# One state chain of four groups in three slots a chunk, V placed beside U by identity products, and TensorE in the written order

## The chip, the cores and the metric

The kernel runs on one core of one Trainium2 chip, in one launch. The metric is the device time of that launch in microseconds (us), lower is better. Engines: PE is TensorE (its queue of weight loads is PEld), DVE is VectorE, ACT is ScalarE, POOL is GpSimd, SP issues most of the DMAs.

## What is computed

A two-layer hybrid backbone over 256 context tokens and 1024 latent tokens of width 1024. Layer 0 runs RWKV-7 time mixing (8 heads, both directions) and an order-2 Hyena long convolution (512 channels) side by side on one input projection; layer 1 is differential attention; each ends with a mixture of experts. The change lies in layer 0. The time mixing is a recurrence on a 64x64 state per head and direction:

```python
def step(s, inp):
    r_t, w_t, k_t, v_t, kk_t, a_t = inp
    sa = jnp.einsum('bhij,bhj->bhi', s, kk_t)
    s = (s * w_t[:, :, None, :]
         - sa[..., None] * (kk_t * a_t)[:, :, None, :]
         + v_t[..., None] * k_t[:, :, None, :])
    return s, jnp.einsum('bhij,bhj->bhi', s, r_t)
...
z = x1 * (fft_long_conv(v, kf[:, 0]) + v * hy_b[0])
return x2 * (fft_long_conv(z, kf[:, 1]) + z * hy_b[1])
```

The filters `kf` of the Hyena come from a small network, times a decay, divided by the sum of their absolute values, and transformed to frequencies.

## The kernel before

**The recurrence in chunks.** Tokens go in 40 chunks of 32 (C), two of them (WIN) a window, 20 windows (NW). The 8 heads are four groups of two; a head (h) and a direction (d) of a group is a quad, 32 partitions of a tile. Before the chain, each group is prepared (`rw_prep`): per chunk the arrays ar, G, bt, and T, the inverse of a triangular 32x32 matrix. `inverses` (L807) makes T on DVE by back substitution, 60 dependent ops on tiles N and Xt, and sends it to DRAM.

**The chain** (`rw_chain`, L870) loads a window's ar, G, T, bt, and V into one half of the tile uv, by SP. Then per chunk: pA, 16 products of G with V, copied by ACT to gv; then, for each of two chains of two groups (NS, GS): pr, the decayed state, on POOL; 8 products of ar with the state S into pc; rh on DVE; 8 products of T with rh; four copies of 32x128 of the result U into the other half of uv, two by DVE (L923) and two by ACT; 8 products of bt with uv, where U and V lie below one another in 64 partitions; and the new S on DVE, L141 (the shared line of all tensor_tensor ops). Last, pY: 32 products of G with uv and of ar with the old S add up to the chunk's output, which ACT copies to yw and SP stores. An fp32 product is two records in the trace.

**The fill** (`fill`, L2003) is what runs beside the chain: the rest of the input projection (`rest`, L685: the Hyena's columns i = 3 to 11, tile pj, which DVE mixes over neighbouring tokens into u, and the last inverses), the Hyena's filters (`filt`, L398, tile fps), the Hyena itself (`stage_hy`, tile hps), and steps of the adaLN projection (adaps). All large products are in three parts of an fp32r split, high x high, low x high and high x low (L171 to L173).

A filter's values are made in a loop over j (L426 to L441): two products of 512 columns, fbt on DVE, and on POOL two adds into nacc and two into EO; after 2 or 8 j the sum nacc is reduced by a product with ones (L443), by which all values are then scaled.

```python
self.tt(self.g, na, na, ab[:, 0], OP.add)
self.tt(self.g, na, na, ab[:, 1], OP.add)
self.tt(self.g, Eo[:, 0, j], fbt[:, 0], fbt[:, 1], OP.add)
self.made = self.tt(self.g, Eo[:, 1, j], fbt[:, 0], fbt[:, 1], OP.subtract).ins
yield 4
```

**What sets the order.** `weave` (L1998) steps through two lists of generators, the chain with the readout behind it (`rw_out`) and the fill, and always takes the one that has done the smaller share of its total: 64 (RWN) against 2509. What a generator yields is counted as done. This gives the order in which the program is written. The order on each engine is then set by a scheduler that simulates the program's times (`schedule_with_timeline_sim=True`, L2077), PE included.

Of the kernel before, what the change touches and what calls it, by code (L numbers as in the profile page):

```python
# [10 lines left out]
F32 = mybir.dt.float32  # L11
# [14 lines left out]
C = 32  # L26
NCH = NT // C
WIN = 2
# [94 lines left out]
class Net:  # L123
# [274 lines left out]
    def filt(self, p1, pw, pv, tabs, pp):  # L398
# [8 lines left out]
        for seg, (j0, nt) in enumerate(((0, 2), (2, 8))):  # L407
            for o in range(2):
                E = []
                for half in range(2):  # L410
# [71 lines left out]
    def filt_lat(self, pv, tabs, pw, pp, E, o):  # L482
# [3 lines left out]
        for cls in range(4):  # L486
            th, tl = next(tabs)
            for Eo, rn, cs in E:
                ko = pw.tile([128, 5, 256], F32, name="ko", bufs=1)
                for e in range(2):  # L490
# [9 lines left out]
                    yield 24 if cls else 12  # L500
# [16 lines left out]
class Net2(Net):  # L517
# [34 lines left out]
    def proj(self, w_src, ncol, hi, lo, wp, pp, toks, evac):  # L552
        raw = wp.tile([128, 8, 128], F32, name="wraw", bufs=1)
        self.sy.dma_start(raw[:, :, :ncol], w_src.rearrange("(k p) n -> p k n", p=128))
        wh = wp.tile([128, 8, 128], F32R, name="whi")
        wl = wp.tile([128, 8, 128], F32R, name="wlo")
        self.split(wh[:, :, :ncol], wl[:, :, :ncol], raw[:, :, :ncol])
        for t0, n in toks:
            ps = pp.tile([128, 512], F32, name="pj")
            self.mm3(ps[:ncol, :n], [((wh[:, k, :ncol], wl[:, k, :ncol]), (hi[:, k, t0:t0 + n], lo[:, k, t0:t0 + n])) for k in range(8)])  # L560
            evac(ps[:ncol, :n], t0, n)
# [38 lines left out]
    def stage_a2(self, pools, er, wp, hi, lo, pp):  # L600
# [23 lines left out]
        def run(c0, ncol, out, w0, w1, w2, b=None):  # L624
# [4 lines left out]
            self.proj(win[:, c0:c0 + ncol], ncol, hi, lo, wp, pp, TOK3,  # L629
# [26 lines left out]
        def hyena(i, bp, pt):  # L656
            u = up.tile([128, GG], F32, name="u")
            run(RWC + 128 * i, 128, u, self.c("cw", i), self.c("cw", 12 + i), self.c("cw", 24 + i), self.c("cb", i))
# [34 lines left out]
        return rest()  # L693

# [150 lines left out]
NS = 2  # L845
GS = 4 // NS
RPA = 1
# [3 lines left out]
class Net3(Net2):  # L851
# [3 lines left out]

    def rw_chains(self, es):
        a, v, g = self.a, self.v, self.g
        self.dram("y", [2, 2, GG, 4, 64])
        self.rp = self.pool(es, "rw", 2, side="right")
        self.rq = q = self.pool(es, "rwq", 2, side="right")  # L860
        self.rps = self.pool(es, "rwp", 1, PSUM, side="right")
        st = []
        for s in range(NS):
            x = q.tile([128, 2, GS, 64], F32, name=f"S{s}")
            v.memset(x, 0.0)
            st.append(x)
        for w in range(NW):
            st = yield from self.rw_chain(w, st)

    def rw_chain(self, w, st):  # L870

        v, g, pe, dr, p, q = self.v, self.g, self.pe, self.dr, self.rp, self.rq
# [4 lines left out]
        uv = p.tile([128, 2, WIN, 4, 64], F32, name="uv")  # L877
        yw = p.tile([128, WIN, 4, 64], F32, name="yw", bufs=1)
        for d in range(2):
# [3 lines left out]
            for h in range(2):  # L883
# [3 lines left out]
                self.sy.dma_start(uv[r0:r0 + 32, d].rearrange("s i g v -> s i (g v)"),  # L887
# [3 lines left out]
        quads = [(qd, qd // 2, qd % 2, slice(32 * qd, 32 * qd + 32), slice(64 * (qd // 2), 64 * (qd // 2) + 64)) for qd in range(4)]  # L891
        for i in range(WIN):
            ps = self.rps.tile([128, 4, 64], F32, name="pA", bufs=RPA)
            for gr in range(4):
                for qd, h, d, qs, hs in quads:
                    ms = slice(64 * h + 32 * (1 - d), 64 * h + 32 * (1 - d) + 32)
                    pe.matmul(ps[qs, gr], G[ms, d, gr, i, 0:C], uv[ms, d, i, gr], start=True, stop=True, tile_position=(ms.start, 32 * qd))
            gv = q.tile([128, 4, 64], F32, name="gv")
            self.act(gv, ps, AF.Copy)
            new = []  # L900
            for s in range(NS):
                gs = range(GS * s, GS * s + GS)
                S = st[s]
                pr = q.tile([128, 2, GS, 64], F32, name=f"pr{s}", bufs=1)
                for d in range(2):
                    db = self.dcoef[:, GS * s:GS * s + GS, d, CS[d][w] + i].unsqueeze(2).to_broadcast([128, GS, 64])
                    self.tt(g, pr[:, d], S[:, d], db, OP.mult)
                ps = self.rps.tile([128, GS, 64], F32, name=f"pc{s}")
                for j, gr in enumerate(gs):
                    for qd, h, d, qs, hs in quads:  # L910
                        pe.matmul(ps[qs, j], ar[hs, d, gr, i, 0:C], S[hs, d, j], start=True, stop=True, tile_position=(64 * h, 32 * qd))
                rh = q.tile([128, GS, 64], F32, name=f"rh{s}", bufs=1)
                self.stt(v, rh, ps, -1.0, gv[:, GS * s:GS * s + GS], OP.mult, OP.subtract)
                ps = self.rps.tile([128, GS, 64], F32, name=f"pc{s}")
                for j, gr in enumerate(gs):
                    for qd, h, d, qs, hs in quads:
                        pe.matmul(ps[qs, j], T[qs, i, gr], rh[qs, j], start=True, stop=True, tile_position=(32 * qd, 32 * qd))
                for qd, h, d, qs, hs in quads:
                    o = uv[qs, d, i, GS * s:GS * s + GS]
                    if qd % 2:  # L920
                        self.act(o, ps[qs], AF.Copy)
                    else:
                        v.tensor_copy(o, ps[qs])  # L923
                ps = self.rps.tile([128, 2, GS, 64], F32, name=f"pc{s}")
                for d in range(2):
                    for j, gr in enumerate(gs):
                        for h in range(2):
                            hs = slice(64 * h, 64 * h + 64)
                            pe.matmul(ps[hs, d, j], bt[hs, d, i, gr], uv[hs, d, i, gr], start=True, stop=True)
                x = q.tile([128, 2, GS, 64], F32, name=f"S{s}")  # L930
                self.tt(v, x, ps, pr, OP.add)
                new.append(x)
            ps = self.rps.tile([128, 4, 64], F32, name="pY")
            for gr in range(4):
                for qd, h, d, qs, hs in quads:
                    pe.matmul(ps[qs, gr], G[hs, d, gr, i, C:], uv[hs, d, i, gr], start=True, stop=False, tile_position=(64 * h, 32 * qd))
                    pe.matmul(ps[qs, gr], ar[hs, d, gr, i, C:], st[gr // GS][hs, d, gr % GS], start=False, stop=True, tile_position=(64 * h, 32 * qd))
            self.act(yw[:, i], ps, AF.Copy)
            st = new
            if i < WIN - 1:  # L940
                yield 1
        for qd, h, d, qs, hs in quads:
            c0 = CS[d][w]
            self.sy.dma_start(dr["y"][d, h, C * c0:C * (c0 + WIN)].rearrange("(i t) g v -> t i (g v)", t=C), yw[qs].rearrange("t i g v -> t i (g v)"))
        yield 1
        return st
# [66 lines left out]
class Net4(Net3):  # L1013
# [15 lines left out]
    def spec(self, p, pp, th, tl, hi, lo, tiles, yh, yl):  # L1029

        for ks, cr, ci, kr, ki, kr2, re, im in tiles:
# [3 lines left out]
            self.cmul(p, ps, kr, ki, kr2, yh, yl, re, im)  # L1035
            yield 6 * len(ks)
# [80 lines left out]
    def hy_lat(self, p, pw, tabs, pp):  # L1117
# [7 lines left out]
        for o in range(2):  # L1125
# [4 lines left out]
            for cls in (0, 2, 1, 3):  # L1130
# [18 lines left out]
                for acc, (yh, yl) in zip(accs, ys):  # L1149
                    av = acc.rearrange("p (m a) w -> p m a w", m=2) if o else acc.rearrange("p (a b) w -> p b a w", b=2)  # L1150
                    for m in range(2):
# [9 lines left out]
                        self.stage2(cls, av[:, m], ps[:, 0], ps[:, 1], pw, W)  # L1161
                        yield 24 if cls else 12
# [819 lines left out]
class Weave:  # L1982
    RWN = 64
# [19 lines left out]
def fill(net, es, rest):  # L2003
# [3 lines left out]
    with ExitStack() as es:  # L2007
        pp = net.pool(es, "fillp", 3, PSUM)
# [73 lines left out]
```

## Time and profile before

| | |
|---|---|
| median of 3 runs | 4129.59 us (4128.44 to 4133.65) |
| the profiled execution | 4128.25 us, span 4126.4 us |
| mean granted clock of PE | 0.934 |
| busy: DVE, ACT, POOL | 2876.1, 1881.8, 1033.5 us |
| DMA | 858.90 MB, mean 208 GB/s |

The profiled execution is one of the kernel's ordinary runs. The span counts from its first to its last instruction. Busy shares are averages over stages of different kinds; the stage of the change is cut out in the rows below. There a matmul's own duration is longer than the distance to the next one, since they are pipelined: costs on PE are read from start to start. A record with a number behind it (x32) stands for that many of one kind in a row.

### The profile page before, as it was taken

To read this page: it belongs to the slowest core of one execution; us is meant where nothing else is said; L and a number is where in the kernel's file an instruction comes from. 1 tells how busy PE (TensorE), PEld (TensorE's weight loads), DVE (VectorE), ACT (ScalarE), POOL (GpSimd) and SP (SyncE) were. 2 spreads that over 40 slices of the span, in tenths; PEclk is the share of its full clock that TensorE was granted. 3 is DMA by queue.
4 is the path that set the end of the run, shared out by engine and by line. 5 is a ranking of instruction groups with operands and counts; after the bars stand their busy time and mean duration, and the time that the engine had idled before them with its cause. 6 is when DMAs were issued, how large, how long until landed. Compare 5 with 4: busy or idle time off the path is not lost.

```text
span 4126.4 us, 75212 instructions
## 1 busy us (share of the span) xinstructions
PE 3731.2 (90%) x29980; PEld 2949.6 (71%) x29980; DVE 2876.1 (70%) x4269; ACT 1881.8 (46%) x3029; POOL 1033.5 (25%) x1186
## 2 busy tenths in 40 slices
PE   7988888789898999799999997989999787999996
PEld 4866666557677887577777776778887675777775
DVE  5378887556656775577777775157777646899997
ACT  4344443233322222165656664244444421777775
POOL 1165553263523441201111101212223111011100
PEclk9988998789798999799999998999999997999998
DMA  5234346666566677578878874254434545899996
GB/s 162 65 110 123 101 111 186 184 199 196 146 204 215 196 267 243 184 265 291 297 285 292 300 280 135 93 123 113 122 99 118 184 165 214 326 383 382 383 369 215
DMA packets 532010, 858.90 MB, mean 208 GB/s; under 512 B 161665, under 2 KB 337563, under 8 KB 527050
## 3 DMA queue, kind: packets, MB, share of 16 engines
q1 hardware_dynamic: 508704, 754.97, 54.4%
q0 software_dynamic: 19904, 90.55, 7.7%
q10 hardware_dynamic: 3050, 8.56, 0.5%
q8 instruction: 236, 3.87, 0.4%
q14 instruction: 116, 0.95, 0.1%
HBM read 708.00 MB, written 145.95 MB: 207 GB/s over the span
## 4 chain that ended last, share of the span: by engine, by line
PE 52%; issue 18%; DVE 13%; DMA 6%; POOL 5%; ACT 3%; SPq 1%; ACTq 0%; DVEq 0%; POOLq 0%
PE pj L171 4%; PE pj L173 4%; PE pj L172 4%; PE S L1828 3%; PE ps L1405 3%; PE ps L1406 3%; PE ps L1404 3%; DVE mx L1809 2%; PE ops L171 2%; PE ops L172 2%; PE ops L173 2%; PE py L1405 1%; PE py L1404 1%; PE py L1406 1%; PE tps L1824 1%
## 5 line engine op out<-in xcount | busy, mean ns | idle before, releaser
L141 DVE TENSOR_TENSOR wrl<-wr,wrh 128x1024 fp32r<-128x1024 f32 x762 | 924.2, 1223 | 202.1 <-ACT wrh L144 169.7
L144 ACT ACTIVATE wrh<-wr 128x1024 fp32r<-128x1024 f32 x768 | 811.6, 1062 | 376.8 <-PE ps L1406 257.9
L1405 PE MATMUL ps<-wrl,xh 128*128 128x512 f32 x1024 | 410.3, 401 | 5.8 <-DVE wrl L141 5.5
L1404 PE MATMUL ps<-wrh,xh 128*128 128x512 f32 x1024 | 406.8, 399 | 2.0 <-ACT xh L144 1.4
L1406 PE MATMUL ps<-wrh,xl 128*128 128x512 f32 x1024 | 400.8, 391 | 0.0
L171 PE MATMUL pj<-hhi,whi 128*128 128x512 f32 (+3 forms) x944 | 357.8, 380 | 4.8 <-ACT qraw L144 3.3
L172 PE MATMUL pj<-hlo,whi 128*128 128x512 f32 (+3 forms) x944 | 352.2, 373 | 2.8 <-POOL hlo L141 2.3
L173 PE MATMUL pj<-hhi,wlo 128*128 128x512 f32 (+3 forms) x944 | 348.5, 370 | 1.9 <-DVE wlo L141 1.8
L1809 DVE TENSOR_REDUCE mx<-S 128x1 f32<-128x1280 f32 x128 | 185.2, 1486 | 116.8 <-PE S L1808 113.7
L1502 POOL DMA_INDIRECT x<-yo,idx x32 | 72.7, 2273 | 716.8 <-DVE yo L153 716.8
L1405 PEld LDWEIGHTS ps<-wrl,xh 128*128 128x128 f32 x1024 | 193.2, 189 | 55.1 <-DVE wrl L141 18.3
L1404 PEld LDWEIGHTS ps<-wrh,xh 128*128 128x128 f32 x1024 | 193.0, 188 | 55.0 <-issue 12.8
L1406 PEld LDWEIGHTS ps<-wrh,xl 128*128 128x128 f32 x1024 | 193.2, 189 | 37.5
L171 PEld LDWEIGHTS pj<-hhi,whi 128*128 128x128 f32 (+1 forms) x944 | 181.2, 192 | 37.5 <-issue 6.0
L1405 PE MATMUL py<-wrl,hh 128*128 128x512 f32 x512 | 206.7, 404 | 0.0
L1404 PE MATMUL py<-wrh,hh 128*128 128x512 f32 x512 | 204.4, 399 | 2.3 <-DVE yo L153 2.3
L172 PEld LDWEIGHTS pj<-hlo,whi 128*128 128x128 f32 (+1 forms) x944 | 181.4, 192 | 33.7 <-issue 4.9
L173 PEld LDWEIGHTS pj<-hhi,wlo 128*128 128x128 f32 (+1 forms) x944 | 180.7, 192 | 34.2 <-DVE wlo L141 3.8
L1406 PE MATMUL py<-wrh,hl 128*128 128x512 f32 x512 | 201.0, 393 | 0.0
L144 ACT ACTIVATE w<-S,mx 128x1280 f32<-128x1280 f32 x64 | 85.1, 1330 | 240.5 <-DVE mx L1809 240.5
L1327 POOL DMA_INDIRECT xg<-xn,idx x48 | 51.3, 1068 | 528.8 <-PE mtp L1334 476.3
L141 POOL TENSOR_TENSOR qraw<-qraw,cos 128x512 f32<-128x512 f32 x32 | 47.1, 1473 | 409.6 <-DVE qsw L1758 260.8
(426 smaller groups left out, 9082.1 us busy)
## 6 DMA issues: line engine op xcount, KB each, us to landing
wr<-in_moe_w_dram SPq DMA_DIRECT2D x384, 1024.0 KB
adaw<-in_ada_w_dram SPq DMA_DIRECT2D x160, 256.0 KB
tb<-tab_tf_dram POOLq DMA_DIRECT2D x12, 2048.0 KB, 9.2
K<-ks SPq DMA_DIRECT2D x16, 1280.0 KB
G<-G SPq DMA_DIRECT2D x72, 256.0 KB
wraw<-in_ev_w_in_dram SPq DMA_DIRECT2D x25, 512.0 KB
tb<-tab_ti_dram POOLq DMA_DIRECT2D x6, 2048.0 KB, 9.5
bt<-vts SPq DMA_DIRECT2D x80, 128.0 KB
```

The lines of the kernel that those rows point to most:

```text
L141: return e.tensor_tensor(out, a, b, op=op)
L144: return self.s.activation(out, in_, f, **k)
L171: self.pe.matmul(ps, ah, bh, start=start and i == 0, stop=False)
L172: self.pe.matmul(ps, ah, bl, start=False, stop=False)
L173: self.pe.matmul(ps, al, bh, start=False, stop=stop and i == n - 1)
L1327: self.g.indirect_dma_start(out=xg[:cap], out_offset=None, in_=self.dr[f"xn{r}"], in_offset=bass.IndirectOffsetOnAxis(ap=idx[:, e:e + 1], ...
L1404: self.pe.matmul(ps[:, n], x[0], w[0][:, ns], start=k == 0, stop=False)
L1405: self.pe.matmul(ps[:, n], x[0], w[1][:, ns], start=False, stop=False)
L1406: self.last = self.pe.matmul(ps[:, n], x[1], w[0][:, ns], start=False, stop=k == 7).ins
L1502: g.indirect_dma_start(out=self.dr["x0"], out_offset=bass.IndirectOffsetOnAxis(ap=idx[:, e:e + 1], axis=0), in_=yo, in_offset=None, comput ...
L1809: v.tensor_reduce(mx[:, c:c + 1], sc, AX.X, OP.max, negate=True)
L1828: pe.matmul(po[:, m], wT[:, j], V[:, k + j], start=k + j == 0, stop=k + j == 9)
```

## The change

- **One chain** of four groups in the place of two chains of two: pr two POOL ops of 128x256 a chunk, rh one DVE op of 128x256, S one of 128x512, uv one DVE copy of 128x512 (L936 of the changed kernel) in the place of eight of 32x128.
- **V beside U.** V has its own tile vw (`rw_load`). Per chunk, 16 products of vw with pieces of the identity matrix put V into the same PSUM tile as T's products put U (L931), so that one copy fills uv. These are 640 products more.
- **Three slots a chunk** (`yield 1 / 3`): in the first the products with S, rh, and the outputs pY of the chunk before, in the second the identity products, T's products, uv and the next chunk's pA, in the third the products with bt and S. The loads of a window are issued in the first slot of the window before.
- **PE in the written order** in the weave (`manual_schedule`); the other engines stay with the scheduler. The pieces are finer: a projection tile is written in two halves of its sum, a filter or spectrum tile in two parts. Hyena columns 3 to 7 are projected before the weave, 8 to 11 in steps inside it. Totals 54 against 3740, j counts 8 in the place of 4, each adaLN step 6, and the fill has four PSUM buffers in the place of three.

```diff
-NS = 2
-GS = 4 // NS
-RPA = 1
...
+        win = self.rw_load(0)
+        gv = self.rw_within(win, 0, q, pp)
...
         for w in range(NW):
-            st = yield from self.rw_chain(w, st)
...
+            nxt = None
+            for i in range(WIN):
+                ar, G, T, bt, vw = win
+                pr = q.tile([128, 2, 4, 64], F32, name="pr", bufs=1)
+                for d in range(2):
+                    self.tt(g, pr[:, d], S[:, d], self.dcoef[:, :, d, CS[d][w] + i].unsqueeze(2).to_broadcast([128, 4, 64]), OP.mult)
+                ps = pp.tile([128, 4, 64], F32, name="pc")
+                for gr in range(4):
+                    for qd, h, d, qs, hs in quads:
+                        pe.matmul(ps[qs, gr], ar[hs, d, gr, i, 0:C], S[hs, d, gr], start=True, stop=True, tile_position=(64 * h, 32 * qd))
+                rh = q.tile([128, 4, 64], F32, name="rh", bufs=1)
+                self.stt(v, rh, ps, -1.0, gv, OP.mult, OP.subtract)
+                if late:
+                    outputs(*late)
+                    if i == 0:
+                        store(w - 1, late[-1])
+                if i == 0:
+                    yw = p.tile([128, WIN, 4, 64], F32, name="yw", bufs=1)
+                    if w + 1 < NW:
+                        nxt = self.rw_load(w + 1)
+                yield 1 / 3
+                ps = pp.tile([128, 2, 4, 64], F32, name="pc")
+                for gr in range(4):
+                    for qd, h, d, qs, hs in quads:
+                        pe.matmul(ps[qs, 1 - d, gr], self.ident[qs, qs], vw[qs, i, gr], start=True, stop=True, tile_position=(32 * qd, 32 * qd))
+                for gr in range(4):
+                    for qd, h, d, qs, hs in quads:
+                        pe.matmul(ps[qs, d, gr], T[qs, i, gr], rh[qs, gr], start=True, stop=True, tile_position=(32 * qd, 32 * qd))
+                uv = q.tile([128, 2, 4, 64], F32, name="uv")
+                v.tensor_copy(uv, ps)
+                if i < WIN - 1:
+                    gv = self.rw_within(win, i + 1, q, pp)
+                elif nxt:
+                    gv = self.rw_within(nxt, 0, q, pp)
+                yield 1 / 3
+                ps = pp.tile([128, 2, 4, 64], F32, name="pc")
+                for d in range(2):
+                    for gr in range(4):
+                        for h in range(2):
+                            hs = slice(64 * h, 64 * h + 64)
+                            pe.matmul(ps[hs, d, gr], bt[hs, d, i, gr], uv[hs, d, gr], start=True, stop=True)
+                late = (win, i, S, uv, yw)
+                S = q.tile([128, 2, 4, 64], F32, name="S")
+                self.tt(v, S, ps, pr, OP.add)
+                yield 1 / 3
+            win = nxt
...
-                        yield 4
+                        yield 8
...
                 for i in range(3, 12):
-                    hyena(i, bp, pt)
-                    yield 5
+                    if i == 8:
+                        yield 0
+                    yield from hyena_steps(i, bp, pt) if i >= 8 else self.at_once(hyena_steps(i, bp, pt))
...
-    RWN = 64
+    RWN = 54
+    FILL = 3740
...
-        pp = net.pool(es, "fillp", 3, PSUM)
+        pp = net.pool(es, "fillp", 4, PSUM)
...
+                done += 6
+                w += 6
...
-            weave(Weave(Weave.RWN, net.stage_rw(), net.rw_read()), Weave(2509, fill(net, e2, rest)))
+            next(rest)
+            with tc.manual_schedule(engines={mybir.EngineType.PE}):
+                weave(Weave(Weave.RWN, net.stage_rw(), net.rw_read()), Weave(Weave.FILL, fill(net, e2, rest)))
```

How the instructions move. The names in the rows are the tiles above; x16 is that many in a row.

PE in the middle of the chain, before: products of both chains, pY (L936, L937), bt (L929), adaLN and filter values in ones and twos.

```order
L268 MATMUL adaps<-adaw,sT 32x128 x4
L917 MATMUL pc_10485<-rh_10483,T 32x64 x8
L917 MATMUL pc_10523<-rh_10521,T 32x64 x8
L268 MATMUL adaps<-adaw,sT 32x128 x3
L936 MATMUL pY<-uv,G 32x64
L937 MATMUL pY<-S_10304,arw 32x64
L936 MATMUL pY<-uv,G 32x64
L937 MATMUL pY<-S_10304,arw 32x64
L897 MATMUL pA<-uv,G 32x64
L431 MATMUL fps<-fwh,hd 128x512
L431 MATMUL fps<-fwl,hd 128x512
L936 MATMUL pY<-uv,G 32x64
L937 MATMUL pY<-S_10304,arw 32x64
L929 MATMUL pc_10498<-uv,bt 64x64 x8
```

After, the second and third slot of a chunk:

```order
L173 MATMUL hps<-vh,tb 128x256
L931 MATMUL pc<-vw,ident 32x64 x16
L934 MATMUL pc<-rh,T 32x64 x16
L985 MATMUL pA<-vw,G 32x64 x16
L171 MATMUL hps<-vh,tb 128x256
L172 MATMUL hps<-vl,tb 128x256
L173 MATMUL hps<-vh,tb 128x256
L171 MATMUL hps<-vh,tb 128x256
```

and, seven rows further,

```order
L172 MATMUL hps<-vl,tb 128x256
L173 MATMUL hps<-vh,tb 128x256
L947 MATMUL pc<-uv,bt 64x64 x16
L171 MATMUL hps<-yh,tb 128x256
```

The products of one step of the chain now stand together, with 12 to 24 fill products between the steps; the identity products (L931) are new.

PE at the end of a filter's loop j, before: the product L443 stands behind some 60 rows of chain products that come after the last j.

```order
L911 MATMUL pc_10271<-S_10073,arw 32x64 x8
L911 MATMUL pc_10309<-S_10111,arw 32x64 x8
L897 MATMUL pA<-uv,G 32x64 x12
L917 MATMUL pc_10282<-rh_10280,T 32x64 x8
L897 MATMUL pA<-uv,G 32x64
L917 MATMUL pc_10320<-rh_10318,T 32x64 x8
L897 MATMUL pA<-uv,G 32x64 x2
L443 MATMUL fps<-nacc,ones 128x256
L431 MATMUL fps<-fwh,hd 128x512
```

After, it stands directly behind the last j:

```order
L896 MATMUL pY<-uv,G 32x64 x4
L898 MATMUL pY<-S,arw 32x64 x4
L896 MATMUL pY<-uv,G 32x64 x4
L898 MATMUL pY<-S,arw 32x64 x4
L431 MATMUL fps<-fwh,hd 128x512
L431 MATMUL fps<-fwl,hd 128x512
L443 MATMUL fps<-nacc,ones 128x256
L171 MATMUL fps<-vh,tb 128x256
L172 MATMUL fps<-vl,tb 128x256
L173 MATMUL fps<-vh,tb 128x256
```

What was between the last j and L443 now stands ahead of them.

DVE in the last group's inverse (N, Xt), before: the mixes u of the Hyena's columns, on 128x1312, stand between its steps.

```order
L141 TENSOR_TENSOR Xt_5922<-N_5921 128x234
L596 TENSOR_SCALAR u_6933<-raw_6934,pcol_94 128x1312
L141 TENSOR_TENSOR N_5921<-N_5921,Xt_5922 128x13x18
L153 SCALAR_TENSOR_TENSOR u_6933<-raw_6934,pcol_94,u_6933 128x1312
L141 TENSOR_TENSOR Xt_5922<-N_5921 128x228
L153 SCALAR_TENSOR_TENSOR u_6933<-raw_6934,pcol_94,u_6933 128x1312
L141 TENSOR_TENSOR N_5921<-N_5921,Xt_5922 128x12x19
```

After, the same stretch:

```order
L141 TENSOR_TENSOR Xt_5922<-N_5921 128x240
L141 TENSOR_TENSOR N_5921<-N_5921,Xt_5922 128x15x16
L141 TENSOR_TENSOR Xt_5922<-N_5921 128x238
L141 TENSOR_TENSOR N_5921<-N_5921,Xt_5922 128x14x17
L141 TENSOR_TENSOR Xt_5922<-N_5921 128x234
L141 TENSOR_TENSOR N_5921<-N_5921,Xt_5922 128x13x18
L141 TENSOR_TENSOR Xt_5922<-N_5921 128x228
L141 TENSOR_TENSOR N_5921<-N_5921,Xt_5922 128x12x19
```

The u mixes that were between the inverse's steps now stand ahead of the inverse or behind it.

## Rows read from the trace of the kernel before

**Rows 1.** page, busy time, share of the span and instructions of each engine

```profile
PE 3731.2 (90%) x29980; PEld 2949.6 (71%) x29980; DVE 2876.1 (70%) x4269; ACT 1881.8 (46%) x3029; POOL 1033.5 (25%) x1186
```

**Rows 2.** windows: stretch, length, busy of each engine (instructions), PEclk, DMA share, GB/s

```profile
714.00:1368.00 654.00, 562.02 (x9669) 443.16 (x9672) 393.83 (x896) 197.84 (x470) 272.62 (x410) 0.85 0.65 190
1368.00:1552.00 184.00, 166.22 (x1197) 144.45 (x1197) 139.41 (x282) 48.34 (x102) 74.54 (x95) 0.94 0.78 246
1307.00:1368.00 61.00, 58.18 (x1090) 52.30 (x1092) 39.18 (x103) 16.64 (x46) 26.41 (x43) 0.97 0.66 206
1024.70:1081.30 56.60, 48.56 (x813) 31.17 (x811) 30.66 (x61) 22.36 (x49) 44.03 (x62) 0.74 0.44 129
```

**Rows 3.** timelines of DVE and PE: start, duration, engine, line [idle before <-releaser]

```profile
670.65 0.20 DVE L141 TENSOR_TENSOR Xt<-N 128x30 f32<-128x30 f32 x1 [5.01 <-DMA N<-G]
695.99 0.96 DVE L596 TENSOR_SCALAR u<-raw,pcol 128x1312 f32<-128x1312 f32 x1 [1.42 <-DMA bt<-bt]
697.18 1.58 DVE L153 SCALAR_TENSOR_TENSOR u<-raw,pcol,u 128x1312 f32<-128x1312 f32 x1
...
708.15 0.19 DVE L141 TENSOR_TENSOR N<-N,Xt 128x30 f32<-128x30 f32 x1
...
714.36 0.21 PE L917 MATMUL pc<-rh,T 32*32 32x64 f32 x1
...
1367.64 0.89 DVE L141 TENSOR_TENSOR S<-pc,pr 128x256 f32<-128x256 f32 x2
...
1552.38 1.22 PE L171 MATMUL ops<-owh,yh 128*128 128x512 f32 x2 [3.55 <-ACT owh L144]
```

**Rows 4.** waits between 714 and 1368: total us, times, longest us

```profile
ACT uv L144 <- DVE uv L923: 96.0, 91, 6.5
DVE uv L923 <- PE pc L917: 37.5, 27, 8.2
PE pA L897 <- DMA uv<-vt: 33.7, 17, 6.5
PEld pA L897 <- DMA G<-G: 26.1, 8, 6.7
DVE rh L153 <- PE pc L911: 19.1, 17, 4.2
```

**Rows 5.** timeline of PE through one chunk, columns as in rows 3

```profile
1309.65 0.28 PE L172 MATMUL hps<-yl,tb 128*128 128x256 f32 x1
1309.77 0.28 PE L173 MATMUL hps<-yh,tb 128*128 128x256 f32 x1
1309.98 0.65 PE L911 MATMUL pc<-S,arw 64*32 64x64 f32 x32
1310.56 0.39 PE L171 MATMUL hps<-yh,tb 128*128 128x256 f32 x1
...
1314.58 0.65 PE L917 MATMUL pc<-rh,T 32*32 32x64 f32 x32
1315.16 0.39 PE L173 MATMUL hps<-yh,tb 128*128 128x256 f32 x1
...
1318.94 1.15 PE L929 MATMUL pc<-uv,bt 64*64 64x64 f32 x32
1320.02 0.34 PE L936 MATMUL pY<-uv,G 64*32 64x64 f32 x8
...
1320.89 0.33 PE L911 MATMUL pc<-S,arw 64*32 64x64 f32 x9
```

**Rows 6.** groups of POOL, 714 to 1368: busy us, mean ns, idle before

```profile
L141 POOL TENSOR_TENSOR EO<-fbt 128x256 f32<-128x256 f32 x80 | 65.8, 841 | 37.7 <-DVE fbt L434 21.4 <-DVE fbt L141 16.2
L141 POOL TENSOR_TENSOR nacc<-nacc,abt 128x256 f32<-128x256 f32 x80 | 63.1, 789 | 17.5 <-ACT abt L144 16.2
```

**Rows 7.** groups of DVE: uv (714 to 1368), wT (whole span)

```profile
L923 DVE COPY uv<-pc 32x128 f32<-32x128 f32 x160 | 44.8, 281 | 54.5 <-PE pc L917 37.5 <-ACT uv L144 15.0
...
L1835 DVE COPY wT<-tps 128x512 f32<-128x512 f32 x128 | 87.9, 687 | 56.1 <-PE tps L1824 56.1
```

More of the change, by code (lines that the diff above doesn't have):

```diff
@@ L559, in proj @@
             ps = pp.tile([128, 512], F32, name="pj")
-            self.mm3(ps[:ncol, :n], [((wh[:, k, :ncol], wl[:, k, :ncol]), (hi[:, k, t0:t0 + n], lo[:, k, t0:t0 + n])) for k in range(8)])
-            evac(ps[:ncol, :n], t0, n)
+            for k0 in (0, 4):
+                self.mm3(ps[:ncol, :n], [((wh[:, k, :ncol], wl[:, k, :ncol]), (hi[:, k, t0:t0 + n], lo[:, k, t0:t0 + n])) for k in range(k0, k0 + 4)],
+                         k0 == 0, k0 == 4)
+                if k0:
+                    evac(ps[:ncol, :n], t0, n)
+                yield 12 * n / 256
     def stage_a(self, es):
@@ L622, in stage_a2, with run, run_steps @@
         self.sy.dma_start(g2, a["rw_g2"][0])
-        def run(c0, ncol, out, w0, w1, w2, b=None):
+        def run(*args):
+            for _ in run_steps(*args):
+                pass
+        def run_steps(c0, ncol, out, w0, w1, w2, b=None):
             raw = rp.tile([128, GG + 2], F32, name="raw")
@@ L654, in stage_a2, with hyena, hyena_steps @@
         self.act(wa[:64], wa[:64], AF.Tanh)
-        def hyena(i, bp, pt):
+        def hyena(*args):
+            for _ in hyena_steps(*args):
+                pass
+        def hyena_steps(i, bp, pt):
             u = up.tile([128, GG], F32, name="u")
-            run(RWC + 128 * i, 128, u, self.c("cw", i), self.c("cw", 12 + i), self.c("cw", 24 + i), self.c("cb", i))
+            yield from run_steps(RWC + 128 * i, 128, u, self.c("cw", i), self.c("cw", 12 + i), self.c("cw", 24 + i), self.c("cb", i))
             kind, ch = divmod(i, 4)
@@ L854, in stage_rw @@
             yield from self.rw_chains(es)
+    QUADS = [(qd, qd // 2, qd % 2, slice(32 * qd, 32 * qd + 32), slice(64 * (qd // 2), 64 * (qd // 2) + 64)) for qd in range(4)]
     def rw_chains(self, es):
-        a, v, g = self.a, self.v, self.g
+        v, g, pe, dr = self.v, self.g, self.pe, self.dr
         self.dram("y", [2, 2, GG, 4, 64])
-        self.rp = self.pool(es, "rw", 2, side="right")
-        self.rq = q = self.pool(es, "rwq", 2, side="right")
-        self.rps = self.pool(es, "rwp", 1, PSUM, side="right")
@@ L862, in rw_chains @@
[L862 to L866, printed above, removed]
-        for w in range(NW):
-            st = yield from self.rw_chain(w, st)
-    def rw_chain(self, w, st):
-        v, g, pe, dr, p, q = self.v, self.g, self.pe, self.dr, self.rp, self.rq
+        self.rp = p = self.pool(es, "rw", 2, side="right")
+        q = self.pool(es, "rwq", 2, side="right")
+        pp = self.pool(es, "rwp", 1, PSUM, side="right")
@@ new lines, in rw_chains, with outputs @@
+        S = q.tile([128, 2, 4, 64], F32, name="S")
+        v.memset(S, 0.0)
+        quads = self.QUADS
+        win = self.rw_load(0)
+        gv = self.rw_within(win, 0, q, pp)
+        yw, late = None, None
+        def outputs(win, i, S, uv, yw):
+            G, ar = win[1], win[0]
+            ps = pp.tile([128, 4, 64], F32, name="pY")
+            for gr in range(4):
+                for qd, h, d, qs, hs in quads:
+                    pe.matmul(ps[qs, gr], G[hs, d, gr, i, C:], uv[hs, d, gr], start=True, stop=False, tile_position=(64 * h, 32 * qd))
+                for qd, h, d, qs, hs in quads:
+                    pe.matmul(ps[qs, gr], ar[hs, d, gr, i, C:], S[hs, d, gr], start=False, stop=True, tile_position=(64 * h, 32 * qd))
+            self.act(yw[:, i], ps, AF.Copy)
@@ L873, in rw_chain, with rw_load @@
+        outputs(*late)
+        store(NW - 1, yw)
+        yield 1 / 3
+    def rw_load(self, w):
+        dr, p = self.dr, self.rp
         ar = p.tile([128, 2, 4, WIN, 64], F32, name="arw")
@@ L890, in rw_chain @@
                                   dr["bt"][d, h, 64 * c0:64 * (c0 + WIN)].rearrange("(i s) g k -> s i (g k)", s=64))
[L891 to L946, printed above, removed]
+        return ar, G, T, bt, vw
+    def rw_within(self, win, i, q, pp):
+        G, vw = win[1], win[4]
+        ps = pp.tile([128, 4, 64], F32, name="pA")
+        for gr in range(4):
+            for qd, h, d, qs, hs in self.QUADS:
+                ms = slice(64 * h + 32 * (1 - d), 64 * h + 32 * (1 - d) + 32)
+                self.pe.matmul(ps[qs, gr], G[ms, d, gr, i, 0:C], vw[ms, i, gr], start=True, stop=True, tile_position=(ms.start, 32 * qd))
+        gv = q.tile([128, 4, 64], F32, name="gv")
+        self.act(gv, ps, AF.Copy)
+        return gv
```

36 lines of the change are left out of this document (26 added, 10 removed).

## The prediction

> **What bounds the kernel now.** I read the page's first part, then the windows, then single timelines in one stage, then the waits. TensorE (PE) is busy 3731.2 of 4126.4 us [rows 1], but the change acts in one stretch only. The first product with T starts at 714 us, the last sum S at 1368 [rows 3]: in between, the state chain runs woven with the fill. From there to 1552 us, where the output projection starts [rows 3], the rest of the Hyena runs alone. In the windows [rows 2] PE is idle for 654.0 - 562.0 = 92 us between 714 and 1368, and its granted clock is 0.85. With two levels, full and half, 0.85 is 30% of the time at half, 196 us, which at full clock would have been 98 us shorter. Dense work at full clock is thus about 654 - 92 - 98 = 464 us: the bound there is not PE's products but the gaps, and the clock that goes with them. The end of the chain, 1307 to 1368, is different: 2.8 us idle in 61, clock 0.97. There the fill is long and even, and PE hardly waits.
>
> The waits [rows 4] say where the gaps come from: uv is copied by two engines that wait for each other (ACT 96.0 us behind DVE's copies), pA waits for its window's V and G (33.7 and 26.1 us), DVE waits for PE's pc (37.5 us for uv).
>
> **What a chunk costs PE in the written order.** One chunk of before, at 1310 us, happens to run almost as the change writes it [rows 5]: the two chains' products side by side, Hyena products between. The time from a row's start to the next row's start is what its products cost at full clock: 32 with S 0.58 us (1309.98 to 1310.56), 32 with T 0.58, 32 with bt 1.08, the 64 of pY about 1.05 (1320.02 to 1320.89, where the first products with S are mixed in, so rounded up). The 32 of pA have T's shape: 0.58. The change adds 32 identity products a chunk. **No row shows them**; the nearest is T's, the same 32x32 pieces into the same kind of tile, so 0.58 again. Bounds: 0.3 (half, if they ran together with T's) and 1.1 (as bt's). Sum 4.45 us. A change of kind costs 0.21 instead of 0.12 (1309.77 to 1309.98), so 0.1 extra: six changes between chain and fill a chunk, 0.6, and some four inside the blocks at up to 0.2, 0.8. So 5.85 a chunk, for 40 of them **234 us**.
>
> **The fill inside the chain.** By the order of the changed program: 824 fps and 744 hps products of 256 columns at 0.12 [rows 5], 188 us; 192 pj of 512 columns at twice that and 72 of 256, 55 us; 80 fps of 512 columns for the filters' values, 19 us; 584 short adaps products, between T's 18 ns and bt's 34 ns each, at most 20 us. That is **282 us**, with the chain 516 us, 12.9 a chunk. As a test against before's 464 us: pj adds 55, 89 more hps 11, identity 23, together 553, so that 37 us would have to go in changes of kind, which before are on every few products.
>
> **What lies on top.**
> - *The filters' values (loop j).* Each j gives POOL two nacc and two EO ops: 2 x 0.789 + 2 x 0.841 = 3.26 us [rows 6]. The written order puts 16 j into 8 slots (2.7 chunks), twice, in halves of 8 with the product with nacc (L443) right behind the last of each. POOL needs 16 x 3.26 = 52 us and 4 to 5 for pr, 57 in all, while PE has 2.7 x 12.9 = 34 to do. PE must wait for the last nacc: +23, twice, **+46**. Before, the stretch with 16 j, 1024.7 to 1081.3, took 56.6 us as well [rows 2], with POOL busy 44.0 and clock 0.74. Bounds: 0 (POOL's work spreads over its neighbours) and 2 x 30.
> - *Gaps and half clock elsewhere.* By the window 1307 to 1368: 2.8 idle in 61 is 5%, clock 0.97 is 6% at half, 3% lost; I take 10% of the 447 us that are not loop j, **+45**. Bounds: 0, and as between 714 and 1368 of before, (92 + 98)/464 = 41%, 183 us.
> - *The ends.* The last outputs now come after the last S, and the first chunk waits for its loads with nothing to interleave: **+10**, between 0 and 20 (a chunk and a half).
>
> Chain: 516 + 46 + 45 + 10 = **617 us** instead of 654.
>
> **DVE, ACT, POOL.** DVE and ACT lose 160 copies of 32x128 each, on DVE 44.8 us; DVE gains 40 copies of 128x512, at wT's 0.69 us [rows 7] 28 us. I count **nothing** for busy time: neither engine is full (393.8 and 197.8 of 654 us [rows 2]). What counts is what covers each wait. uv has pA and 12 or more fill products (2 us) between T and bt for its 0.69 us and DVE's queue; rh has pY and a fill piece; S, a sum of the same size as uv, has one fill piece of 1.4 to 2.9 us: the thinnest cover of the three. The queue holds ops of 0.7 to 1.6 us, so some slots wait; that is inside the 45. If the cover were gone everywhere, it would be rival 2. The DMA queues issue as many loads as before, vw's in uv's place.
>
> **The chain starts earlier.** T of the last group comes from DVE's inverse, 670.65 to 708.15 [rows 3]. Between its ops stand nine u mixes, three of 0.96 and six of 1.58 us, 12.4 us, and the queue waits for two of them (one 1.42 us). The order shows none of them inside the inverse now: **-14**, first product with T at about 700. Bounds: 0, if what feeds the inverse comes later, and -15. 264 pj products leave this stretch too, but there PE is merely kept filled.
>
> **The tail** has 89 hps less, 11 us: 184 - 11 = **173**.
>
> End of the stage: 700 + 617 + 173 = 1490 instead of 1552.4: -62 us. Behind it nothing is moved. The profiled run took 4128.25 (span 4126.4), so 4066; the median of the runs is 1.3 higher, so **4067 us**.
>
> **Rivals.**
> 1. *Denser, chance 0.20.* PE waits little for POOL and half of the 45 goes too: chain 540 to 550, about 3996. For it: 1307 to 1368 already has this form. Against it: L443 stands fixed in the written order.
> 2. *Slower, chance 0.14: PE in the written order stands behind DVE's queue.* Before, the scheduler put any ready product into a gap; now rh, uv or S late by 1 us holds up every fill product behind it, and the fill feeds the very ops that are late. There are 120 slots. It decides from a chain of 654 + 14 + 11 = 679 us, (679 - 516)/120 = 1.4 us a slot over dense. At 2 us a slot the chain takes 756 and the time is 4206. For it: rh waited 19.1 and uv 37.5 us for PE, one of them 8.2 [rows 4], DVE is 60% busy, and the clock falls where PE stalls. Against it: the covers above, and 1307 to 1368.
> 3. *Loads late, chance 0.05.* A window's loads are issued four slots, some 17 us, before its pA, and 59.8 us were waited for V and G before [rows 4]. If that stays, behind PE's fixed order, the chain is 677 and the time 4127: no change.
> 4. *Row tiles on one bank, chance 0.01.* T's row shows products of four row tiles into one tile of PSUM, 18 ns apart. If the 1280 new ones ran one after the other, at the 0.21 us of a single one [rows 3], that would be 269 us instead of 23, and about 4313. The Trainium skill, TensorEngine Tiling (Array Packing), Gotcha 1: PSUM Pressure, says that different row tiles cannot access the same PSUM bank simultaneously, which would speak against this change; T's row doesn't agree with it.
> 5. *The change doesn't do what it says, chance 0.03:* the other engines' orders, still the scheduler's, hold the chain at today's 16.3 us a chunk: 4128 - 14 - 11 gives 4103 if start and tail gain, 4128 if not.
>
> **How the numbers follow.** The forecast (chain 590 to 645) has 0.57. The measurement tells 0.2%, 8 us, from no change. Faster: 0.57 + 0.20 + 0.02 of the last, 0.79; same 0.06 (loads, and the rest of the last); slower 0.15. The range goes from 3990 (denser) to 4138 (loads late, and the mild end of the stalls); most of rival 2, rival 4 and the end of rival 1 lie outside.
>
> **What would show it.** In the changed profile: first product with T near 700 us, last S near 1317, output projection near 1490; in between PE idle 50 to 90 us, half of it before L443, the clock over 0.9; no waits for uv on ACT; POOL busy through both stretches of j. It would be wrong if T's first product came no earlier, if the gaps stood before the products with T, bt and S instead of L443 (rival 2), or if pA waited for DMA for over 50 us (rival 3).

## The result and the profile after

The changed kernel takes 4237.48 us (median of 4 runs, 4231.25 to 4242.66), the kernel before 4131.62 beside it: a ratio of 1.0249, 95% interval 1.0227 to 1.027. It is **slower** by 2.5%; 4067 had been forecast, with 4138 as the upper end. The profiled execution is one of 4235.4 us, span 4233.6.

The page's busy line and three windows of the changed kernel: chain, tail, and the dense end of the chain (columns as in [rows 2]).

```profile
PE 3656.8 (86%) x31260; PEld 2910.6 (69%) x31260; DVE 2863.3 (68%) x4068; ACT 1838.4 (43%) x2869; POOL 1016.9 (24%) x1106
```

```profile
701.00:1428.00 727.00, 522.48 (x11313) 444.50 (x11314) 396.35 (x729) 161.15 (x326) 263.28 (x350) 0.85 0.60 175
1428.00:1668.00 240.00, 177.55 (x1114) 143.63 (x1113) 139.49 (x263) 48.03 (x97) 69.79 (x84) 0.85 0.58 185
1317.00:1428.00 111.00, 105.51 (x2577) 95.94 (x2573) 64.19 (x141) 22.82 (x55) 46.87 (x64) 1.00 0.75 228
```

PE is busy for 74 us less than before [rows 1] in a span that is 107 us longer. The chain, from the first product with T at 701.3 to the last S at 1427.9, takes 726.6 us instead of 654; the output projection starts at 1667.7, so the tail is 240 instead of 184. Idle time of PE in the chain went from 92 us [rows 2] to 204.5. Behind the stage nothing was lost: 4233.6 - 1667.7 = 2566 us, against 2574 before.

What the prediction had said of the start is there: DVE's inverse runs from 667.3 to 693.1 (it took 37.7 us with the u mixes in it [rows 3]), and T's first product is at 701.3.

Timelines of DVE and PE of the changed kernel, columns as in rows 3:

```profile
667.33 0.20 DVE L141 TENSOR_TENSOR Xt<-N 128x30 f32<-128x30 f32 x1 [3.27 <-DMA N<-G]
...
692.93 0.19 DVE L141 TENSOR_TENSOR N<-N,Xt 128x30 f32<-128x30 f32 x1
...
701.34 0.41 PE L934 MATMUL pc<-rh,T 32*32 32x64 f32 x2 [5.29 <-DMA T<-xt]
```

The waits of PE alone, between 701 and 1428:

```profile
PE fps L443 <- POOL nacc L141: 100.8, 8, 18.0
PE hps L171 <- ACT vh L144: 31.7, 2, 21.4
PE pc L947 <- DVE uv L936: 16.0, 7, 6.0
PE pc L916 <- DVE S L141: 15.8, 8, 3.9
...
PE pc L931 <- DVE rh L153: 0.5, 2, 0.3
```

In the kernel before, PE's wait at the same product, between 714 and 1368, was

```profile
PE fps L443 <- POOL nacc L141: 4.8, 3, 2.4
```

Half of the idle time of the changed chain stands before this one product, eight times. What the chain itself makes PE wait for, uv, S and rh, is 32 us together, in 120 slots. Two of the eight in PE's timeline (the bracket is the idle time before the row):

```profile
1073.08 1.22 PE L443 MATMUL fps<-nacc,ones 128*128 128x256 f32 x2 [17.54 <-POOL nacc L141]
...
1109.87 1.22 PE L443 MATMUL fps<-nacc,ones 128*128 128x256 f32 x2 [16.79 <-POOL nacc L141]
```

What the engines do in such a wait, in two windows (columns as in [rows 2]): the one that ends at 1073.1, in a latent filter, and the one that ends at 809.1, in the context's first:

```profile
1055.50:1073.10 17.60, 0.06 (x2) 0.02 (x1) 6.99 (x9) 5.45 (x10) 15.78 (x21) 0.60 0.26 78
800.40:809.10 8.70, 0.07 (x2) 0.01 (x1) 1.99 (x3) 2.45 (x5) 3.31 (x5) 0.64 0.27 88
```

POOL, the last of the five engines, works through the first and mostly idles in the second. Over all eight waits it is busy 86 of 102 us.

A chunk in the dense end, also from PE's timeline, shows the chain as written:

```profile
1383.30 0.65 PE L916 MATMUL pc<-S,arw 64*32 64x64 f32 x32
1383.77 0.29 PE L896 MATMUL pY<-uv,G 64*32 64x64 f32 x8
...
1384.77 0.39 PE L171 MATMUL hps<-vh,tb 128*128 128x256 f32 x1
...
1387.83 0.65 PE L931 MATMUL pc<-vw,ident 32*32 32x64 f32 x32
1388.30 0.46 PE L934 MATMUL pc<-rh,T 32*32 32x64 f32 x20
...
1389.19 0.39 PE L171 MATMUL hps<-vh,tb 128*128 128x256 f32 x1
...
1390.82 1.15 PE L947 MATMUL pc<-uv,bt 64*64 64x64 f32 x32
1391.90 0.39 PE L171 MATMUL hps<-yh,tb 128*128 128x256 f32 x1
```

The 32 records of the products with S take 0.47 us, the 32 of the identity products 0.47 (an fp32 product is two records, so these are 16 products each; the prediction counts records). pY takes 1.00 (1383.77 to 1384.77), T's products and pA together 0.89, bt 1.08: 3.9 us of chain products in all, changes of kind between them and to the fill included. From S to S a chunk takes 12 to 16 us there.

### The profile page after: what moved, and what is told of

Its sections match the earlier page's. It is cut to its first block, busy times and chain, and to the rows that moved or that the text cites. A ratio compares the mean times of both kernels' runs of the same rounds, so it can differ in the third digit from the quotient of the medians.

```text
span 4233.6 us, 77213 instructions
## 1 busy us (share of the span) xinstructions
PE 3656.8 (86%) x31260; PEld 2910.6 (69%) x31260; DVE 2863.3 (68%) x4068; ACT 1838.4 (43%) x2869; POOL 1016.9 (24%) x1106
## 4 chain that ended last, share of the span: by engine, by line
PE 53%; DVE 7%; DMA 2%; ACT 2%; issue 2%; POOL 0%; SPq 0%; DVEq 0%; ACTq 0%; POOLq 0%
PE ps L1449 5%; PE ps L1448 5%; PE ps L1450 5%; PE pcx L1458 4%; PE S L1872 3%; PE py L1449 3%; PE py L1448 3%; PE py L1450 3%; PE pj L173 2%; PE pj L171 2%; PE pj L172 2%; PE ops L171 2%; PE ops L172 2%; PE ops L173 2%; DVE mx L1853 2%
## 5 line engine op out<-in xcount | busy, mean ns | idle before, releaser
L1851 PE MATMUL S<-K,Q 128*128 128x512 f32 (+1 forms) x384 | 137.8, 366 | 10.9 <-DMA Q<-qs 10.5
```

The lines of the kernel that those rows point to most:

```text
L1851: pe.matmul(sc[:, k0:k1], Q[:, c], K[:, c, k0:k1], start=True, stop=False)
```

## The experiments

The question: is it the written order of PE, and if so, which places of it; or is one chain of four groups slower by itself?

**1. PE's order given back to the scheduler.**

```diff
-            with tc.manual_schedule(engines={mybir.EngineType.PE}):
+            if True:
```

> The changed kernel, but PE's order in the weave is the scheduler's again, as before; the one chain, the identity products, the slots and the pieces stay. Theory A (PE in the written order stops at fill products whose data other engines still make: 101 us before L443, 32 us at two hps products, 22 us at rpv in the tail, and half clock behind each): nearly all of that goes, the chain takes 600 to 640 us, the tail 175 to 190, the time is 4060 to 4110. Theory B (one chain of four groups is by itself slower than two interleaved chains): the chain stays above 690 us and the time above 4180.

Measured: 4131.63 us, ratio to before 0.9992 (0.9978 to 1.0006); chain 651.0, tail 186.6. Neither theory had it: the written order costs the whole 106 us, but one chain under the scheduler is not faster than two, so the 4060 to 4110 did not come. L443's wait is down to 2.0 us; PE's longest waits, between 718 and 1369, are

```profile
PE pA L985 <- DMA G<-G: 36.9, 14, 7.2
PE pc L947 <- DVE uv L936: 15.6, 11, 4.1
PE adaps L268 <- DMA adaw<-in_ada_w_dram: 14.3, 12, 3.9
PE pc L916 <- DVE S L141: 12.6, 6, 4.4
```

Each is small; the sum of idle time is 138 us, and 137 us of PE's busy time lies at half clock, where the written order has 98. The chain here also holds less work: the scheduler puts the 264 records of projection products (pj) that the written order has inside the chain ahead of it, as in the kernel before, and T's first product comes at 718.2 instead of 701.3.

**2. The kernel before in the written order.** Its `weave` is put under the same `manual_schedule`, nothing else.

> The kernel before with its two chains and coarse pieces, and PE in the written order in the weave. Theory A: the order's fixity is what costs, so waits of PE for fill data and now also for the chain's own rh, uv and S show, over 250 us of idle PE between the first product with T and the last S, and the time is 4250 to 4500. Theory B: about as before, 4110 to 4160.

Measured: 4606.27 us (one run), chain 1094.5. PE's waits between 678 and 1773:

```profile
PE pc L929 <- ACT uv L144: 136.7, 80, 6.2
PE pc L917 <- DVE rh L153: 91.1, 79, 9.4
PE fps L443 <- POOL nacc L141: 64.6, 8, 12.8
```

With two chains and coarse pieces, a fixed order does what rival 2 said: PE stands behind the chain's own uv, here ACT's copies, and DVE's rh, about 80 times each. The time is even past the 4500 of theory A. Part of the longer chain is work (512 us at full clock, against 473 in the changed kernel): the projection of all nine columns lies in this `weave`, where the changed kernel has four.

**3. The coarse pieces of the fill put back, in the written order.**

```diff
-                yield 12 * n / 256
+                if k0:
+                    yield 24 * n / 256
```

and in the same way, twice as much at half as many places, for filters and spectra.

> The changed kernel with the old, coarse pieces of the fill (a projection tile, a filter tile, a spectrum tile in one piece), PE in the written order as in the change. The kernel before in the written order took 4606, the changed one 4237. If the pieces make the difference, 4400 to 4600. If the one chain in slots makes it, 4230 to 4290.

Measured: 4269.18 (one run). The pieces give 32 of the 369 us from 4606 to 4237; the other 337 come with the rest of the change: the one chain in three slots, but also the columns projected ahead of the `weave`, the new totals and counts and the fourth PSUM buffer. No run parts these, so that the one chain gives most of it is likely but not shown.

**4. L443 made free of POOL's nacc; then the adds into nacc left out too.**

```diff
-                    self.pe.matmul(ps[:, :256], self.ones, na, start=True, stop=True)
+                    self.pe.matmul(ps[:, :256], self.ones, dl, start=True, stop=True)
```

> The changed kernel, but the product L443 reads the decay rates instead of nacc, so it needs nothing from POOL; all of POOL's work, the two adds into nacc too, stays. The filters are scaled by something else than the sum of their absolute values. Place theory (L443 stands too early in PE's fixed order, and what stands behind it doesn't need nacc): the 101 us before L443 go, under 40 us turn up elsewhere, the time is 4130 to 4175. Throughput theory (POOL needs 3.26 us a j wherever PE stops): 60 us or more of the wait turn up at the next products that need EO or a free fbt, the time is 4195 to 4240.

> As the run with L443 free, and the 80 adds into nacc are left out (POOL 1.7 us a j). Throughput theory: POOL is then no longer behind PE, and against the run with L443 free another 50 to 90 us go; the time is 4120 to 4160. Place theory: no more than 25 us between the two.

Measured: 4195.7 and 4168.99 (one run each). Chain 685.9 and 658.4, tail 239.8 in both. By its time alone the throughput theory has the first (60 us or more of waits moved, 4195 at the lowest). Free of nacc, 41 us of the chain go; idle time falls by 43 us only, so nearly 60 us of waits move to what comes next in the order. PE's longest waits of the first of the two (the first row is as in the changed kernel, the other vh row was 1.6 there, the table's load tb 2.4, and fbt was not among its waits):

```profile
PE hps L171 <- ACT vh L144: 31.7, 2, 21.0
PE fps L171 <- ACT vh L144: 20.4, 3, 7.4
PE fps L431 <- DVE fbt L141: 18.5, 8, 5.2
...
PE fps L171 <- DMA tb<-tab_tfc_dram: 15.8, 1, 15.8
```

Without POOL's adds another 27.5 go, where one theory had 50 to 90 and the other under 25. So both theories hold a part: in this order of the edits the place gives about 41 and POOL's adds behind it 27, together 68 us of chain for the 101 us of wait. The split depends on the order: as long as L443 waits for nacc, POOL's work is what it waits for.

**5. The adds into nacc on DVE, alone; with the readout in pieces; and with a slot of the chain before L443.**

```diff
-                        self.tt(self.g, na, na, ab[:, 0], OP.add)
-                        self.tt(self.g, na, na, ab[:, 1], OP.add)
+                        self.tt(v, na, na, ab[:, 0], OP.add)
+                        self.tt(v, na, na, ab[:, 1], OP.add)
```

> The changed kernel with the two adds into nacc moved from POOL to DVE, nothing else. POOL then has 1.7 us a j instead of 3.3, DVE 0.8 more. Theory A: the wait before L443 falls from 101 us to under 35, with the half clock behind it 80 to 110 us go, and the time is 4130 to 4160; the tail stays at 240. If DVE takes POOL's place as what L443 waits for, the wait stays over 70 us and the time over 4200.

> As the run with nacc on DVE, and the readout behind the chain is written in pieces of a third, so that Hyena products stand between its dependent products. Theory A: the 22 us of PE at rpv and 7.5 at rps go, with some half clock: the tail falls from 240 to 195 to 215 us, the time is 25 to 45 us under that of the run with nacc on DVE alone. If the tail is long for another reason (the Hyena's own chain through DVE, POOL and ACT), it stays within 10 us of 240.

> The run with nacc on DVE and the readout in pieces, with two further edits: abt has two buffers in the place of one, and in the written order one slot of the chain is put between the last j and its L443 (a j counts 5 instead of 8, and three a j are counted ahead of L443). Theory A (fixed places): the 60 us at L443 fall to under 20, the time from 4191 to 4130 to 4155. If the wait moves to the fps products behind it, the time stays above 4175.

Measured: 4221.29 (ratio 1.0212, 1.0187 to 1.0238), 4191.25 (1.014, 1.012 to 1.0159) and 4180.52 (1.0117, 1.0095 to 1.014). The first missed its 4130 to 4160, and its rival's 70 us of wait: the time is over 4200, but the wait fell to

```profile
PE fps L443 <- DVE nacc L141: 60.0, 8, 11.0
```

and the chain by 31 us. L443 then waits for DVE's queue. One slot of the chain before it, with a second buffer for abt, left 49 us at the same place (the third, a miss too: the time stayed above 4175, but the wait did not move on). The readout did nearly as expected: the time is 30 us under the first (25 to 45 said), the tail fell from 248.5 to 219.4 (195 to 215 said), the wait before rpv from 21.7 to 10.9.

**6. x2c out of vt's buffer.**

```diff
-                        x2 = p.tile([128, NC], F32, name="x2c", tag="vt")
+                        x2 = p.tile([128, NC], F32, name="x2c", bufs=3)
```

> The changed kernel with x2c, the gate of the context's Hyena, in three buffers of its own and no longer in that of vt. PE stands 21 us before the first hps product of the latent Hyena and 10 before that of the context's, and before the former DVE's queue waits three times 5 to 8 us for x2c's loads, one after the other, with vt behind them. If those loads make the 21 us, 15 to 30 us go with the half clock behind them: 4205 to 4222. If vt is late for another reason, within 8 us of 4237.

Measured: 4231.46, ratio 1.0246 (1.0223 to 1.0269), not told apart from the changed kernel. The wait of 31.7 us is down to

```profile
PE hps L171 <- ACT vh L144: 8.9, 1, 8.9
```

and DVE's waits for x2c's loads fell from 18.5 us to 2.3, so these loads did make the longer one, and the chain is 14 us shorter. But the tail is 4 longer and the rest of the kernel 6; what stays is less than the runs can tell.

**7. All three places at once**, in the written order: experiment 4's second kernel, the readout in pieces, x2c's buffers.

> PE in the written order with all three named places taken away at once: L443 reads the decay rates and the adds into nacc are left out (the filters are scaled by something else than the sum of their absolute values), the readout is in pieces, x2c has three buffers of its own. Place theory: the gains add up (4169 for the first alone, 22 to 29 off the tail, 6 to 14 for x2c): 4120 to 4140, level with the kernel before and with the scheduler's order, and the written order has then no price left but no gain either. If the places only hand the wait on to each other, it stays above 4150.

Measured: 4133.75, ratio 1.0011 (0.9997 to 1.0025). The gains add up. This is a kernel that leaves out POOL's 80 adds into nacc, so it draws level with less work. Its chain and tail (columns as in [rows 2]):

```profile
695.00:1332.00 637.00, 516.22 (x11311) 440.06 (x11312) 392.86 (x728) 158.36 (x326) 207.58 (x270) 0.90 0.67 200
1332.00:1557.00 225.00, 171.23 (x1116) 142.58 (x1115) 143.50 (x265) 54.43 (x105) 73.18 (x86) 0.86 0.62 201
```

The chain, 637 us, is still 20 us over the 617 of the prediction, and those held 46 us for L443, which is gone here. Dense work is 474 us as in the changed kernel, so 163 us are idle time (121) and half clock (43), where the prediction had 55 besides L443. The longest wait left, 16.5 us, is for the load of a table. The tail, 225, is still 41 over that of before; 10.6 of these are the router's weights (below), 8.9 the loads of y for the readout, 8.3 what is left before rpv. What makes the rest, in the chain and in the tail, is not settled.

**8. A version that beats both.** From experiment 1's kernel, PE in the scheduler's order: nacc on DVE; then the loads of a window in the order G, vw, ar, T, bt (what pA needs first; the first loop keeps vw, the second has T and bt); then x2c's buffers and a second one for abt.

```diff
         for d in range(2):
             c0 = CS[d][w]
-            self.sy.dma_start(ar[:, d].rearrange("p g c t -> p g (c t)"), dr["ar"][:, d, :, c0:c0 + WIN].rearrange("g p c t -> p g (c t)"))
             self.sy.dma_start(G[:, d].rearrange("p g c t -> p g (c t)"), dr["G"][:, d, :, c0:c0 + WIN].rearrange("g p c t -> p g (c t)"))
             for h in range(2):
...
+        for d in range(2):
+            c0 = CS[d][w]
+            self.sy.dma_start(ar[:, d].rearrange("p g c t -> p g (c t)"), dr["ar"][:, d, :, c0:c0 + WIN].rearrange("g p c t -> p g (c t)"))
+            for h in range(2):
...
```

> The run with the scheduler's order on PE, with the adds into nacc on DVE. If POOL's 3.26 us a j bound the j loops under the scheduler too (they took 56 us for 16 j before), 20 to 50 us go: 4080 to 4112. If the scheduler had covered them, or DVE now takes POOL's place, it stays within 10 us of 4131.

> The run with the scheduler's order and nacc on DVE, with a window's loads written in the order G, vw, ar, T, bt, so that what pA needs is issued first. With the scheduler's order PE waited 37 us for G before pA. If the order of the loads makes that wait, 15 to 35 us go and the time is 4092 to 4112, under both kernels. If G's buffer (freed by the outputs of the window before) makes it, the time stays within 8 us of 4127.

> The run with the scheduler's order, nacc on DVE and the loads in the order G, vw, ar, T, bt (4106), with x2c in three buffers of its own and two buffers for abt. Under the scheduler's order PE waits 6 us for the Hyena's vh and ACT for nacc behind abt; if these still end on PE's path, 5 to 20 us go: 4086 to 4101. If the scheduler covers them, within 8 us of 4106.

Measured: 4127.38 (0.999, 0.9977 to 1.0004), 4106.35 (0.9939, 0.9916 to 0.9963), 4096.16 (0.9928, 0.9904 to 0.9951). Under the scheduler POOL's work on nacc was covered, as the second theory of that run had it. The new order of the loads gave 21 us, as expected, but not mainly at the wait that was expected. PE's waits for loads with nacc on DVE, and then with the new order:

```profile
PE pA L985 <- DMA G<-G: 21.8, 8, 5.5
PE adaps L268 <- DMA adaw<-in_ada_w_dram: 21.3, 6, 10.4
```

```profile
PE pA L988 <- DMA G<-G: 18.5, 8, 4.8
...
PE adaps L268 <- DMA adaw<-in_ada_w_dram: 5.4, 6, 3.3
```

G's wait had fallen from 36.9 us to 21.8 before the loads were touched and fell by 3 more with them; what fell was the wait for the adaLN weights (adaw). Under the scheduler each edit gives PE a new order, so a wait that changes is not yet the edit's own effect. The last step's interval overlaps the one before it. The last kernel is 0.7% under the kernel before, a small gain, but its interval stays clear of 1. Its chain and tail:

```profile
716.00:1338.00 622.00, 501.34 (x10961) 422.26 (x10960) 419.80 (x797) 151.73 (x315) 208.10 (x263) 0.86 0.68 202
1338.00:1525.00 187.00, 156.35 (x1118) 132.27 (x1117) 135.56 (x262) 46.51 (x97) 68.08 (x85) 0.92 0.69 224
```

## Why the prediction was wrong

**The start** was right: first product with T at 701.3 (700 said), for the reason given.

**The dense work** was said to be 516 us; laying the trace's clock over PE's busy time, the changed chain has 522 busy, 98 of it at half clock, so 473 at full. The 43 us too many are the sum of two errors. The chain's products were costed too high: 5.85 us a chunk, where the chunk at 1383 takes 3.9 with its changes of kind, 157 us in 40 chunks instead of 234. The fill's were costed too low: 473 - 157 = 316 us instead of 282. The prediction's own test, 464 us of dense work before, was 11 us low too: it counted all of the half clock against busy time, but 28 of the 201 us at half clock were idle; by the same measure as here it is 475. Rival 4 did not come: the 32 records of identity products, of four row tiles into one PSUM tile, take 0.47 us, 15 ns apart, where one after the other at 0.21 us would be 6.7. The Trainium skill, TensorEngine Tiling (Array Packing), Gotcha 1: PSUM Pressure, says that different row tiles cannot access the same PSUM bank simultaneously; these rows don't agree with it.

**The step that failed first is the term of loop j, +46.** The mechanism was right (POOL 3.3 us a j, L443 directly behind the last one), its size was not: 101 us. The prediction counted the two stretches of 16 j, which came to 66 us (18.0, 13.3, 17.5, 16.8) instead of 46. It left out the context's filters: four more times two j and an L443, 35 us. That it was POOL's work PE stood behind is in the windows: POOL is busy 59 of the 67 us of the four long waits, and 27 of 35 in the four short ones, of which the first, at 809, is mostly a wait for a filter's weights. POOL's work in a long stretch was sized right (56.3 us busy from 882.3 to 949.8 and 54.2 from 1043.7 to 1109.9, 57 said), but these stretches last 67.5 and 66.2 us, since POOL is idle in 11 and 12 of them, for 3.4 behind a loop's first fbt and for 0.7 at a time behind abt. And the place counts: free of nacc, with POOL's work unchanged, 41 us of the chain go (experiment 4).

**The next, and the largest, is the 45 us for gaps elsewhere** (55 with the ends), taken from a stretch where the scheduler had set the order. In the written order the other waits are 204 - 101 = 103 us, and half clock on busy time costs another 49. The chain's own waits, which rival 2 was about, are only 32 of it. The others are fill products behind fill data: hps behind the Hyena's first split (32), fps behind tables, splits and T. Under the scheduler the same one chain waits 4.4 us at that hps product and not 32 (experiment 1).

**The third is the tail, 173 us.** It was costed as before minus 11 us of products, but it lies inside the `weave` too and so in the written order. There PE stands before the readout's last products and the router's:

```profile
PE rpv L1035 <- ACT yb L144: 21.9, 12, 3.4
PE rtb L1251 <- DMA rtw<-in_moe_router_dram: 14.7, 1, 14.7
```

The readout's steps depend on one another through ACT and DVE and were written back to back; in pieces they give back 29 us (experiment 5). PE comes to the router's first product at 1644.4, 5.7 us before the load of its weights is issued (1650.1), and has to wait for 14.7 us, against 2.6 before.

In sum: start +1, dense -43, L443 55 over, other gaps and clock 97 over, tail 67 over, behind the stage -8: 169 us, from the 4066 said for the profiled execution to its 4235.

Of the signs that were named, half of the idle time does stand before L443, but of 204 us and not of 50 to 90, and the clock is 0.85 and not over 0.9: the share came true while the sum did not.

**Rival 2 had the right sign and the right head, PE's fixed order, but the wrong place.** It watched the chain, where each wait is covered (rh 0.5 us, S and uv 16 each, 0.27 us a slot where 1.4 would decide). That the coverage comes with the change is shown by experiment 2, where two chains in the written order wait 137 and 91 us for uv and rh; which part of the change gives it is not. The forecast then took "the covers hold" for the whole stage.

**Rivals 1, 3 and 5** fell: the chain was dense in stretches only (PE is busy 46 of 50 us from 1000 to 1050 and 19 of the next 50); pA waited for no DMA in the written order; the change did what it says.

## What to carry to other kernels

A fixed order on one engine has to be priced at every instruction whose data comes through other engines, above all at the ends of loops (a sum, a reduction, a readout written back to back), not only on the path that the change is about: list them in the written order, take the latency of each from its producers' rows, and ask what stands between. A chain of work that is covered step by step still loses if its cover is itself a chain. What a scheduler covers and what it doesn't can be seen by giving it the new structure alone: here that run showed no gain, and another order of a window's loads was then worth 0.5%.

## What was not expected of the hardware

In the chain PE's busy time, with what lies at half clock counted half, is 475 us before, 473 after, and 444 under the scheduler with one chain, which has the projection's 264 records ahead of the chain. The idle time more than doubled with the change (92 to 204 us), but busy time at half clock fell from 174 to 98 us. The time at half clock did not fall (201 before, 221 after): before, 28 us of it lay in idle time, after 123, in gaps that are few and long. So with 112 us of new gaps went 38 us less lost in busy time at half clock, (174 - 98)/2, a third of them. Behind the stage, the same instructions took 2566 to 2575 us in these profiled executions, without following where the stage ended: a gain under 10 us in the stage, as that of x2c, can't be read from the whole time of one execution.
